# Two tiles of tokens at once in the second half of q and k and in the second mixer's q

## The chip, the cores and the metric

The kernel runs on one core of one Trainium2 chip. The metric is the device time of one execution in microseconds. The times of before are from three runs; a profile of one more execution gives the trace. Engines are called as in the profile: PE multiplies matrices, PEld is its weight load, DVE, ACT and POOL work on vectors, SP issues the DMAs.

## The reference

A decoder layer for 512 tokens of 1024 channels. One input projection of the normed input yields all parts; two attention mixers run on them; their outputs are gated, merged and projected. Cut to what matters here:

```python
h = rms_norm(x, norm_w)                       # (512, 1024)
proj = h @ w_in                               # all parts from one product
(q_a, k_a, v_a, z_a, q_b, kc, vc, ksl, vsl, kwn, vwn, gate_b, z_b, gate_m) = split(proj)
# first mixer: 8 heads of 64, causal softmax with a relative bias (512 tokens: every block is selected)
o_a = moba_mixer(rms_norm(heads(q_a), q_norm_a), rms_norm(heads(k_a), k_norm_a), heads(v_a), bias_a)
# compressed keys and values: windows of 32 tokens, a two-layer net
k_cmp = rms_norm(compress(heads(kc), ...), k_norm_cmp); v_cmp = compress(heads(vc), ...)
# second mixer: the same q against compressed, selected and window keys, three softmaxes, summed by gates
o_b = nsa_mixer(rms_norm(heads(q_b), q_norm_b), k_cmp, v_cmp, rms_norm(heads(ksl), ...), heads(vsl),
                rms_norm(heads(kwn), ...), heads(vwn), gate_b, bias_b)
y_a = o_a * silu(z_a);  y_b = o_b * silu(z_b);  g_m = sigmoid(gate_m)
merged = g_m[:, :1024] * (y_a @ w_branch_a) + g_m[:, 1024:] * (y_b @ w_branch_b)
x + merged @ w_out
```

## The kernel before

Products of the projections are made in three passes to keep float32's precision: each operand is split in a high part (rounded to the fast format, `hh` of the input, `wh` of a weight) and a low rest (`hl`, `wl`), and high x high, low x high and high x low are added up. ACT makes `wh` by a cast from the loaded weight `wr` (L402), DVE makes `wl` by a subtraction (L412). A "chunk" is 128 input channels by up to 512 columns; there are eight chunks (`KT`) to a group of columns.

There are four tiles of 128 tokens (`NT`). Two kinds of projection exist. A channel product (`gemm_chan`, for kc, vc, the z gates and the merge gates; accumulator `pgc`) holds weights still and streams all 512 tokens. A token product (`gemm_tok`; accumulator `pgt`) holds a tile of tokens still and streams 512 columns. The order of the projections is the list `qk0 v kc vc qk1 za0 kb za1 za2 qb za3 vb zb0 zb1 zb2 zb3`: qk1 is q and k of heads 4 to 7 of the first mixer, qb is the q of the second one. The first of the list, qk0, runs through `gemm_first`, with all four tiles at once in four accumulators (`pgf`). All others go tile by tile:

```python
def gemm_tok(name, emit, tags="gggg"):
    _, per, n = tlay[name]
    ws = W.take(KT // per, n)            # the split of all chunks is asked for here
    for t in range(NT):
        yield room(tags[t])              # an accumulator of this kind must be free
        ps = psum(tags[t], "pgt")
        ...                              # eight chunks x three products, each a step
                elif t == NT - 1:
                    W.split(W.i + i)     # in the last tile: ask for the next weights, a chunk a step
        with_rx(lambda t=t, ps=ps: emit(t, ps))
```

PSUM holds eight accumulators of one bank each: two of kind "g" (channel products, token products, branch products `pbr`), two "s" (scores `sps`), three "t" (small ones, and the compressor's hidden sum `hps`, which holds one for long) and one "o" (the attention outputs `O`).

When the four tiles of qk1 or qb end, `emit` starts a chain of steps for each: ACT evicts the accumulator to `nraw` with the token's scale (L772) and squares it (L774, one buffer `nxn` for all), DVE sums (L775), POOL takes the power -1/2 (L489), DVE multiplies by it and by the gains (L779, L786), ACT and DVE split the result into two half-precision parts (L795, L803, L796, L805, L1033), and after every second tile a DMA transposes it into `qkt` (L245).

Scores (L1094) are read from their bank by DVE (L1114), go through exponentials on ACT (L1125, L1132) and a rest on DVE (L1136), are transposed by DMA into `dst`, and are multiplied with v into `O` (L1168). In between, the compressor `compress_h` multiplies (L940, `hps`), copies its hidden sum to `hs` (L947 on ACT) and multiplies that (`pu`, L952).

All engines' instructions are put in order by a planner in the kernel itself, ahead of time: generators for scores, projections, compression, values and so on yield either a wait or the cost of what they issued, and the planner, with a clock of its own (`now`), takes at each step the one that may go on. An engine executes its queue in that order; semaphores make it wait where a result is missing.

Of the kernel before, what the change touches and what calls it, by code (L numbers as in the profile page):

```python
# [22 lines left out]
P = 128  # L23
NT = S // P
KT = D // P
# [33 lines left out]
SHARE_C = 100.0  # L59
LAG = 20000  # L60
MARGIN = 300
LATE_A = 1000
LATE_V = 2000
LATE_S = 1000
# [44 lines left out]
def hybrid_kernel(ctx: ExitStack, tc: tile.TileContext, x, x0, xT, wtok, wchan, gains, w1,  # L109
                  relone, wbr, wout, consts, out):  # L110
    nc = tc.nc
# [19 lines left out]
    now = [0.0]  # L131
# [26 lines left out]
    def cm(n):  # L158
        return 4.5 + 0.4427 * n
# [105 lines left out]
    def psum(tag, name, dt=F32):  # L265
        return alloc(tag, name, dt=dt)
# [9 lines left out]
    def room(*tags):  # L276

        def f():
            r = 0.0
            for tag in tags:  # L280
                if len(held[tag]) >= RES[tag][1]:
                    t = [z[0] for z in held[tag] if z[0] is not None]
                    if not t:
                        return None
                    r = max(r, min(t))
            return r
        return f
# [170 lines left out]
    first = alloc("dst", "x0", (P, NBLK * P // 2))  # L458
# [12 lines left out]
    hh = cp.tile([P, KT, S], F32R, name="hh")  # L471
    hl = cp.tile([P, KT, S], F32R, name="hl")
# [34 lines left out]
    for _ in range(NWARM):  # L507
        nc.tensor.matmul(pw[:, :P], warm[:, :1].to_broadcast([P, P]), warm[:, :1].to_broadcast([P, P]), start=True,
                         stop=True)
# [33 lines left out]
    def with_rx(fn):  # L543

        if "rx" in done:
            fn()
        else:
            rx_todo.append(fn)
# [45 lines left out]
    tlay, _ = tok_layout()  # L594
# [61 lines left out]
    for j in (5, 6, 2, 3, 4):  # L656
        tiles += right[j]
    W = Stream(tiles, NRAW - 2, lambda: wp.tile([P, WT], F32R, name=nm("wh"), tag="whi"),
               lambda: wp.tile([P, WT], F32R, name=nm("wl"), tag="wlo"))
# [10 lines left out]
    def gemm_tok(name, emit, tags="gggg"):  # L670
        _, per, n = tlay[name]
        ws = W.take(KT // per, n)
        for t in range(NT):
            yield room(tags[t])
            ps = psum(tags[t], "pgt")
            hs = [(hh[:, k, t * P:(t + 1) * P], hl[:, k, t * P:(t + 1) * P], None) for k in range(KT)]
            i = 0
            for c in mm3(ps[:, :n], hs, ws):
                yield c
                if not callable(c):  # L680
                    i += 1
                    if per == 2:
                        ahead((t + i / KT) / NT)
                    elif t == NT - 1:
                        W.split(W.i + i)
            with_rx(lambda t=t, ps=ps: emit(t, ps))

    def gemm_first(name, emit, tags="ggss"):

        _, per, n = tlay[name]  # L690
        ws = W.take(KT // per, n)
        ps = [psum(tag, "pgf") for tag in tags]
        for k in range(KT):
            for a, b in ((0, 0), (1, 0), (0, 1)):
                yield need(f"xl{k}" if a else f"xh{k}")
                if b or not a:
                    yield need((W, b, k // per))
                for t in range(NT):
                    nc.tensor.matmul(ps[t][:, :n], (hl if a else hh)[:, k, t * P:(t + 1) * P], ws[k][b],
                                     start=(k == a == b == 0), stop=(k == KT - 1 and b == 1))  # L700
                    if k == KT - 1 and b:
                        with_rx(lambda t=t: emit(t, ps[t]))
                yield cm(n) * NT
            W.split(W.i + k + 1)
# [112 lines left out]
    def proj_norm(name, first=False, tags="gggg"):  # L817
        two = []

        def emit(t, ps):  # L820
            if not t:
                qk_alloc(name)
            if t % 2 == 0:
                two[:] = [att(name, F32).bitcast(F16) for _ in range(2 + (name[:2] == "qk"))]
            n = 0 if name == "kb" else 2 if name == "qb" else 1
            q, k = two[:n], two[n:]
            ch = Chain(now[0] + 230)
            if name == "kb":
                e_ = sp.tile([P, 24], F32, name=nm("ge"), tag="ge", bufs=3)
                ch.do({"A": 164}, lambda e: e.activation(e_, ps[:, 256:280], AF.Exp, scale=nrx[:, t:t + 1]))  # L830
            norm(ch, ps, t, name, 4 if name == "kb" else 8, q, k)
            if name == "kb":
                def g1(e):
                    e.tensor_scalar(gate[:, 0, :, t], e_, 1.0, 1.0 / PS, op0=ALU.add, op1=ALU.mult)
                    e.reciprocal(gate[:, 1, :, t], gate[:, 0, :, t])
                ch.do({"D": 300}, g1)
            ch.mark(f"{name}.{t}")
        yield from (gemm_first(name, emit) if first else gemm_tok(name, emit, tags))

    def proj_v(name, tags="gggg"):  # L840
        toks[name], per, i = [None] * NT, 1 + (name == "vb"), int(name == "vb")
# [790 lines left out]
    class Run:  # L1632
        def __init__(r, gen, share, margin=MARGIN):
            r.gen, r.share, r.vt, r.wait, r.live, r.margin = gen, share, 0.0, lambda: 0.0, True, margin
# [10 lines left out]
    for k in range(KT):  # L1645
# [3 lines left out]
    now[0] = 3500.0  # L1649
    A, F, C, X, B, V = Run(scores(), SHARE_A, LATE_A), Run(gemms(), SHARE_F), Run(cmp(), SHARE_C, LATE_C), Run(x_rms(), 100.0), Run(prepare(), SHARE_B), Run(  # L1650
        values(), SHARE_V, LATE_V)
# [5 lines left out]
    while any(r.live for r in runs):  # L1657
        live = [r for r in runs if r.live]
        ws = [(r, r.wait()) for r in live]
# [88 lines left out]
```

## Time and profile before

| | |
|---|---|
| runs | 422.29 us median of 3 (421.83 to 422.44) |
| profiled execution | 422.54 us, of which the span in the trace is 420.5 us |
| PE, DVE, ACT, POOL busy | 411.8, 356.3, 297.9, 35.1 us |
| DMA queue of the kernel | 74.86 MB, 70.5% of the 16 engines' span |
| qk1's token products | from 64.57 us to 93.98 us |
| qb's token products | from 131.76 us, between other work |

A row of the timeline gives the start in microseconds, the duration, the engine, the line, the operation, output <- inputs, the shape and how many; in brackets the idle time of the engine before it and who ended it. Products are pipelined: the duration of one overlaps the next, so what a product costs is the distance from its start to the next one's. In the table of windows each engine has its busy time and instructions, and at the end of a row stand the granted clock of PE, the share of DMA and GB/s.

### The profile page before, as it was taken

How to read it: one execution, taken by the hardware profiler on the slowest of the kernel's cores; microseconds unless marked ns; L12 is line 12 of the kernel's file. 1: busy time of each engine (PE TensorE's matmuls, PEld its weight loads, DVE VectorE, ACT ScalarE, POOL GpSimd, SP SyncE). 2: the span in 40 equal slices, each digit the busy share in tenths (PEclk: the TensorE clock that was granted, in tenths of full speed). 3: DMA queues.
4: the chain of work that ended last, by engine and by line, in shares of the span. 5: the costliest groups of instructions: out<-in, count | busy, mean ns of one | idle time of the engine just before them, and what ended most of it. 6: DMA issues, size and time to landing. Idle time of an engine off the chain costs nothing.

```text
span 420.5 us, 7307 instructions
## 1 busy us (share of the span) xinstructions
PE 411.8 (98%) x2235; PEld 322.0 (77%) x2235; DVE 356.3 (85%) x933; ACT 297.9 (71%) x793; POOL 35.1 (8%) x37
## 2 busy tenths in 40 slices
PE   9999998999998999999999999999999999999996
PEld 7877875778976677897766777666777888888885
DVE  5967969999899987778999997899956967698993
ACT  7996748997797988727988897898943433445620
POOL 0015100123210033200000000000000000000000
PEclk9999999999999999999999999999999999999999
DMA  8951785688969988750878778889799597251232
GB/s 278 311 190 49 129 271 140 137 183 214 264 201 232 195 163 194 218 153 12 147 168 196 150 161 200 167 195 160 145 162 348 175 374 278 79 180 44 56 143 100
DMA packets 116693, 75.30 MB, mean 179 GB/s; under 512 B 89072, under 2 KB 92016, under 8 KB 116656
## 3 DMA queue, kind: packets, MB, share of 16 engines
q1 hardware_dynamic: 116656, 74.86, 70.5%
q8 instruction: 17, 0.28, 0.3%
q14 instruction: 20, 0.16, 0.1%
HBM read 51.11 MB, written 2.75 MB: 128 GB/s over the span
## 4 chain that ended last, share of the span: by engine, by line
PE 54%; DVE 23%; DMA 9%; ACT 5%; issue 5%; SPq 1%; POOL 1%; DVEq 0%; ACTq 0%; POOLq 0%
PE pgc L437 21%; PE pbr L437 9%; PE po L437 9%; PE pgt L437 8%; DMA wr<-in_wtok 5%; DVE sb L1114 4%; DVE wl L412 4%; DVE sb L1136 4%; DMA wr<-in_w 3%; PE O L1168 3%; PE sps L1094 3%; ACT wh L402 2%; DVE vl L412 1%; SPq L238 1%; DMA T<-rtab 1%
## 5 line engine op out<-in xcount | busy, mean ns | idle before, releaser
L437 PE MATMUL pgc<-hh,wh 128*128 128x512 f32 x208 | 87.1, 419 | 0.0
L412 DVE TENSOR_TENSOR wl<-wr,wh 128x512 fp32r<-128x512 f32 (+1 forms) x112 | 73.1, 669 | 11.8 <-ACT wh L402 11.6
L437 PE MATMUL pgc<-hh,wl 128*128 128x512 f32 x208 | 81.5, 392 | 0.0
L437 PE MATMUL pgc<-hl,wh 128*128 128x512 f32 x208 | 81.2, 390 | 0.0
L402 ACT CAST wh<-wr 128x512 fp32r<-128x512 f32 (+1 forms) x111 | 64.0, 599 | 11.2 <-DMA wr<-in_wtok 5.6
L1125 ACT ACTIVATE sb<-sb,sst 128x256 f32<-128x256 f32 (+3 forms) x96 | 53.2, 554 | 10.5 <-DVE sst L1114 10.2
L437 PE MATMUL pgt<-wh,hh 128*128 128x512 f32 (+2 forms) x160 | 58.3, 364 | 0.1
L437 PE MATMUL pgt<-wl,hh 128*128 128x512 f32 (+2 forms) x160 | 56.1, 351 | 0.5 <-DVE wl L412 0.4
L437 PE MATMUL pgt<-wh,hl 128*128 128x512 f32 (+2 forms) x160 | 55.8, 349 | 0.0
L1136 DVE SCALAR_TENSOR_TENSOR sb<-sb,sst 128x256 f16<-128x256 f32 (+3 forms) x96 | 51.1, 542 | 4.2 <-ACT sb L1132 3.9
L1114 DVE CUSTOM_DVE_ANT_0 sb<-sps,T,gst 128x512 f32<-128x512 f32 (+3 forms) x96 | 51.2, 541 | 3.5 <-PE sps L1094 1.6
L1132 ACT ACTIVATE sb<-sb,sst 128x256 f16<-128x256 f32 (+3 forms) x96 | 51.4, 552 | 4.0 <-DVE sst L1128 3.7
L437 PEld LDWEIGHTS pgc<-hh,wh 128*128 128x128 f32 x208 | 39.1, 188 | 8.6 <-issue 0.3
L437 PEld LDWEIGHTS pgc<-hh,wl 128*128 128x128 f32 x208 | 39.0, 188 | 8.6
L437 PEld LDWEIGHTS pgc<-hl,wh 128*128 128x128 f32 x208 | 39.2, 189 | 6.5
L1094 PE MATMUL sps<-qkt,qkt 128*128 128x512 f16 (+3 forms) x176 | 38.2, 310 | 1.6 <-DVE sst L1114 1.4
L489 POOL TENSOR_TENSOR nr<-nss,mhalf 128x8 f32<-128x8 f32 (+1 forms) x16 | 29.0, 1819 | 109.4 <-DVE nss L488 47.9
L437 PEld LDWEIGHTS pgt<-wl,hh 128*128 128x128 f32 x160 | 30.1, 188 | 5.5 <-DVE wl L412 1.6
L437 PEld LDWEIGHTS pgt<-wh,hh 128*128 128x128 f32 x160 | 30.2, 189 | 4.3 <-DVE X L912 0.4
L437 PEld LDWEIGHTS pgt<-wh,hl 128*128 128x128 f32 x160 | 30.2, 189 | 3.4
L1094 PEld LDWEIGHTS <-qkt 128*128 128x128 f16 x176 | 11.5, 98 | 21.4 <-issue 18.5
L437 PE MATMUL pbr<-yh,wh 128*128 128x512 f32 x64 | 26.4, 413 | 0.0
(229 smaller groups left out, 746.3 us busy)
## 6 DMA issues: line engine op xcount, KB each, us to landing
wr<-in_wchan SPq DMA_DIRECT2D x52, 256.0 KB, 3.8
wr<-in_wtok SPq DMA_DIRECT2D x36, 256.0 KB, 4.0
wq<-in_wout SPq DMA_DIRECT2D x36, 256.0 KB, 3.1
T<-rtab SPq DMA_DIRECT2D x16, 256.0 KB, 4.0
wr<-in_w SPq DMA_DIRECT2D x16, 256.0 KB, 3.7
wr<-in_wbr SPq DMA_DIRECT2D x16, 256.0 KB, 3.1
xr<-in_x SPq DMA_DIRECT2D x8, 256.0 KB, 5.3
x<-in_xT SPq DMA_DIRECT2D x7, 256.0 KB, 5.8
```

Source lines behind the costliest of these rows:

```text
L238: nc.sync.dma_start(out=dst, in_=src)
L402: e.copy(hi, raw)
L412: c.do(either(n), lambda e, hi=hi, lo=lo, raw=raw: e.tensor_sub(lo, raw, hi.bitcast(F32))).mark((w, 1, i))
L437: nc.tensor.matmul(dst, sts[i][a], mvs[i][b], start=(start and i == a == b == 0), stop=(stop and i == n - 1 and (a, b) == passes[-1]), ski ...
L489: c.do({"p": 700 + 150 * w}, lambda e: e.tensor_tensor(v(dst), v(ss), mhalf[:parts, :w], op=ALU.pow))
L1094: nc.tensor.matmul(sps[:, :n].rearrange("p (t n) -> p t n", n=P), qs, k4[:, x, j, :b + 1], start=not x, stop=bool(x))
L1114: e.tensor_tensor_reduce(z["sb"], sps[:, :L], T[:, S - L:], scale=nrunscale, scalar=3e38, op0=ALU.add, op1=ALU.min, accum_out=st[:, 0, b:b ...
L1125: c.do({"A": 279 + 0.834 * L}, lambda e: e.activation(z["sb"], z["sb"], AF.Exp, bias=st[:, 0, b:b + 1], scale=-1.0, accum_out=st[:, 1, b:b ...
L1132: e.activation(z["pp"][:, :L], z["sb"], AF.Copy, scale=s_)
L1136: c.do({"d": 59 + cd(L)}, lambda e: e.scalar_tensor_tensor(z["pp"][:, L:], z["sb"], s_, z["pp"][:, :L], op0=ALU.mult, op1=ALU.subtract))
L1168: nc.tensor.matmul(out, v[r][kb][:, vi * DH:(vi + 1) * DH], u.moving(kb, pi), start=p.first and kb == vi == pi == 0, stop=p.last and kb == ...
```

## The change

qk1 and qb go through a new function, `gemm_two`, which takes two tiles of tokens at once: for each chunk, the three passes are made for both tiles before the next chunk. The first two tiles take two accumulators of kind "t", the last two take both of kind "g". The next weights are asked for chunk by chunk over the whole second half. The chains of the two tiles of a half are put 1.5 us apart in the planner's time.

```diff
+STAG = 1500
+TWO = dict(qk1="ttgg", qb="ttgg")
...
+    def gemm_two(name, emit, tags):
+
+        _, per, n = tlay[name]
+        ws = W.take(KT, n)
+        for h in range(2):
+            ps = []
+            for tag in tags[2 * h:2 * h + 2]:
+                yield room(tag)
+                ps.append(psum(tag, "pgt"))
+            for k in range(KT):
+                yield ws[k][2].ready
+                for a, b in ((0, 0), (1, 0), (0, 1)):
+                    for i in range(2):
+                        t = 2 * h + i
+                        nc.tensor.matmul(ps[i][:, :n], (hl if a else hh)[:, k, t * P:(t + 1) * P], ws[k][b],
+                                         start=(k == a == b == 0), stop=(k == KT - 1 and b == 1))
+                yield cm(n) * 6
+                if h:
+                    W.split(W.i + k + 1)
+            for i in range(2):
+                Chain(now[0] + i * STAG).call(lambda t=2 * h + i, p=ps[i]: with_rx(lambda: emit(t, p)))
+
...
-        yield from (gemm_first(name, emit) if first else gemm_tok(name, emit, tags))
+        yield from (gemm_first(name, emit) if first else gemm_two(name, emit, TWO[name]) if name in TWO else gemm_tok(name, emit, tags))
```

Up to the first product of qk1 PE's order is unchanged, and behind the last attention output it is again the same; the other engines' orders part a little later and meet at about the same place. In between they are dealt anew. PE at the start of qk1, before (numbers are those of buffers):

```order
L437 MATMUL pgt182_865<-wh126_685,hh_108 128x512
L437 MATMUL pgt182_865<-wh126_685,hl_109 128x512
L437 MATMUL pgt182_865<-wl127_686,hh_108 128x512
L437 MATMUL pgt182_865<-wh129_693,hh_108 128x512
L437 MATMUL pgt182_865<-wh129_693,hl_109 128x512
L437 MATMUL pgt182_865<-wl130_694,hh_108 128x512
```

and PE at the same place after the change:

```order
L704 MATMUL pgt182_865<-wh126_685,hh_108 128x512
L704 MATMUL pgt183_866<-wh126_685,hh_108 128x512
L704 MATMUL pgt182_865<-wh126_685,hl_109 128x512
L704 MATMUL pgt183_866<-wh126_685,hl_109 128x512
L704 MATMUL pgt182_865<-wl127_686,hh_108 128x512
L704 MATMUL pgt183_866<-wl127_686,hh_108 128x512
L704 MATMUL pgt182_865<-wh129_693,hh_108 128x512
L704 MATMUL pgt183_866<-wh129_693,hh_108 128x512
```

A chunk of weights now serves six products in a row and two accumulators. Between these products stand scores: before, after 9, 12, 3, 9, 6, ... token products and mostly one pair at a time, now after 12, 18, 18, 12, 12, two pairs at a time.

PE at the end of qk1, where za0's channel product (`pgc`) begins, before (pgt239 is tile 3; tile 2 was pgt218, 24 products earlier):

```order
L437 MATMUL pgt239_1168<-wl179_862,hh_108 128x512
L437 MATMUL pgt239_1168<-wh180_863,hh_108 128x512
L437 MATMUL pgt239_1168<-wh180_863,hl_109 128x512
L437 MATMUL pgt239_1168<-wl181_864,hh_108 128x512
L437 MATMUL pgc265_1256<-hh_108,wh244_1183 128x512
```

and after the change (pgt201 is tile 2, pgt202 tile 3):

```order
L704 MATMUL pgt201_1011<-wh180_863,hl_109 128x512
L704 MATMUL pgt202_1012<-wh180_863,hl_109 128x512
L704 MATMUL pgt201_1011<-wl181_864,hh_108 128x512
L704 MATMUL pgt202_1012<-wl181_864,hh_108 128x512
L439 MATMUL pgc273_1270<-hh_108,wh215_1041 128x512
```

The two accumulators of kind "g" now both end here, and pgc273 takes over the one of pgt201. ACT's queue around the eviction that frees it, after the change (nraw217 and nraw224 are tiles 0 and 1 in their chains, xs the compressor's input, sb the scores):

```order
L404 CAST wh256_1216<-wr238_1141 128x280
L819 CAST qk1203_1019<-nraw217_1052 128x4x64
L404 CAST wh260_1234<-wr244_1170 128x280
L819 CAST qk1203_1019<-nraw224_1068 128x4x64
L796 ACTIVATE nraw268_1258<-pgt201_1011,rx_94 128x512
L1156 ACTIVATE sb245_1172<-sb245_1172,sst228_1074 128x256
```

and before, around the eviction of the last tile, which frees nothing that PE's next row needs:

```order
L803 CAST qk1200_958<-nraw204_962 128x2x64
L1033 CAST qk1200_958<-nraw204_962 128x2x64
L772 ACTIVATE nraw267_1263<-pgt239_1168,rx_94 128x512
L803 CAST qk1199_957<-nraw220_1054 128x2x64
L774 ACTIVATE nxn268_1264<-nraw267_1263 128x512
```

The eviction now stands behind the first splits of tiles 0 and 1, whose norms must be done. Where qb begins, PE's row `pu` (the compressor's next product, which waits for ACT's copy `hs`), before:

```order
L437 MATMUL pgc383_1776<-hl_109,wh339_1616 128x512
L437 MATMUL pgc383_1776<-hh_108,wl340_1617 128x512
L437 MATMUL pgt407_1878<-wh342_1625,hh_108 128x512
L437 MATMUL pgt407_1878<-wh342_1625,hl_109 128x512
L437 MATMUL pgt407_1878<-wl343_1626,hh_108 128x512
L952 MATMUL pu410_1893<-cst_89,hs395_1853 128x64 x2
```

and after the change:

```order
L439 MATMUL pgc387_1786<-hl_109,wh333_1592 128x512
L439 MATMUL pgc387_1786<-hh_108,wl334_1593 128x512
L439 MATMUL pgc387_1786<-hh_108,wh333_1592 128x512
L439 MATMUL pgc387_1786<-hl_109,wh333_1592 128x512
L439 MATMUL pgc387_1786<-hh_108,wl334_1593 128x512
L976 MATMUL pu390_1804<-cst_89,hs379_1750 128x64 x2
```

It moved ahead of qb's first product, and the last product of the hidden sum (`hps`), which stood six channel and token products and one pair of scores ahead of it, now stands fifteen channel products and two pairs ahead.

## The prediction

> **What bounds the kernel now.** I read the page first, then the table of windows, then the timeline of the TensorE row at the two places that the change touches. On the page, the busy shares, the slices and the chain of waits:
>
> ```profile
> PE 411.8 (98%) x2235; PEld 322.0 (77%) x2235; DVE 356.3 (85%) x933; ACT 297.9 (71%) x793; POOL 35.1 (8%) x37
> DVE  5967969999899987778999997899956967698993
> PEclk9999999999999999999999999999999999999999
> PE 54%; DVE 23%; DMA 9%; ACT 5%; issue 5%; SPq 1%; POOL 1%; DVEq 0%; ACTq 0%; POOLq 0%
> ```
>
> PE is busy 411.8 of 420.5 us at the full granted clock, so 8.7 us is idle; the rest can only shrink if products follow each other more closely. The table of windows (PE, PEld, DVE, ACT, POOL, then clock) says where the idle time is:
>
> ```profile
> 60.00:70.00 10.00, 9.59 (x46) 6.69 (x45) 9.80 (x31) 8.84 (x27) 0.00 (x0) 1.00 0.61 153
> 70.00:80.00 10.00, 8.69 (x39) 5.69 (x38) 9.81 (x32) 7.81 (x29) 0.00 (x0) 1.00 0.64 162
> 130.00:140.00 10.00, 8.53 (x43) 6.22 (x42) 9.63 (x28) 9.78 (x30) 1.01 (x1) 1.00 1.10 223
> 140.00:150.00 10.00, 9.21 (x62) 6.79 (x61) 9.24 (x35) 9.66 (x34) 0.76 (x1) 1.00 0.90 194
> 200.00:240.00 40.00, 39.94 (x242) 28.15 (x241) 39.73 (x124) 35.38 (x105) 0.00 (x0) 1.00 0.84 169
> ```
>
> 0.41 + 1.31 us stand where qk1 begins and 1.47 + 0.79 us where qb begins, each time with DVE above 92%: 4.0 us in exactly the stretches that the diff rewrites. Outside them PE hardly waits, even at 200 to 240 us where DVE has no idle time left. So the question is what these two stretches cost afterwards.
>
> **The change: products themselves, nothing.** 96 products of qk1 and 96 of qb remain, each with its own weight load, 128x512. What changes is that two accumulators alternate. The same alternation, over four, runs in gemm_first:
>
> ```profile
> 10.62 1.07 PE L699 MATMUL pgf<-wh,hh 128*128 128x512 f32 x4
> 11.53 1.07 PE L699 MATMUL pgf<-wh,hl 128*128 128x512 f32 x4
> 64.57 0.39 PE L437 MATMUL pgt<-wh,hh 128*128 128x512 f32 x1
> 64.80 0.39 PE L437 MATMUL pgt<-wh,hl 128*128 128x512 f32 x1
> ```
>
> Four in 0.91 us is 0.228 each; one tile at a time goes at 0.23. Term: 0.
>
> **Term 1, the weights of qk1's first tile.** Before, a chunk of weights is used up in three products (0.68 us), after in six (1.37 us). The first tile of qk1 in the timeline:
>
> ```profile
> 67.97 0.40 PE L437 MATMUL pgt<-wh,hl 128*128 128x512 f32 x1
> 68.75 0.50 PE L437 MATMUL pgt<-wl,hh 128*128 128x512 f32 x1 [0.39 <-DVE wl L412]
> 70.02 0.40 PE L437 MATMUL pgt<-wh,hl 128*128 128x512 f32 x1
> 70.53 0.49 PE L437 MATMUL pgt<-wl,hh 128*128 128x512 f32 x1
> 72.14 0.40 PE L437 MATMUL pgt<-wl,hh 128*128 128x512 f32 x1
> 73.65 0.38 PE L1094 MATMUL sps<-qkt,qkt 128*128 128x256 f16 x2 [1.12 <-DVE sst L1114]
> 74.11 0.50 PE L437 MATMUL pgt<-wh,hh 128*128 128x512 f32 x1
> 74.45 0.39 PE L437 MATMUL pgt<-wh,hl 128*128 128x512 f32 x1
> 68.02 1.28 DVE L412 TENSOR_TENSOR wl<-wr,wh 128x512 fp32r<-128x512 f32 x2
> 72.84 0.75 DVE L1114 CUSTOM_DVE_ANT_0 sb<-sps,T,gst 128x512 f32<-128x512 f32 x1
> ```
>
> From 67.97 to 68.75 is 0.78 instead of 0.23, from 70.02 to 70.53 0.51: 0.83 us lost to chunks 5 and 7, whose low halves DVE had just made. After, PE comes to chunk 5's low half at about 64.57 + 12 x 0.23 + 0.4 (a pair of scores) + 12 x 0.23 + 4 x 0.23 = 71.4; DVE has it at 68.7 (the first of the pair at 68.02). So both waits go: **-0.83**, between -0.83 and 0 (0 if DVE is 2.7 us later than before, which I see no reason for).
>
> **Term 2, the bank of the scores.** At 72.14 PE waits 1.51 - 0.23 = 1.28 us for a score bank, which DVE reads at 72.84 after four chunks of weights and two pairs of scores were asked of it within 8 us. After, two pairs of scores are issued in the same 8 us but with 30 token products between start and the second pair instead of 21, and the chunks stand ahead of the scores in DVE's queue. Walking DVE's queue with the durations above (0.6 a chunk, 0.4 to 0.7 a score), the third pair of scores finds its second bank some 0.4 us late. Term: **-0.9**, between -1.28 and +0.3 (three such waits of 0.4 us, less the 0.9 that I count).
>
> **Term 3, fewer returns from scores to tokens.** A token product that follows scores holds PE longer: 74.11 to 74.45 is 0.34, so 0.11 over the pitch. From the start of qk1 to the end of vb the order has 18 such returns, not 24, because scores now come in fours. Term: 6 x 0.11 = **-0.7**, between -0.7 and 0.
>
> **Term 4, a new wait: za0.** Both banks "g" now hold qk1's tiles 2 and 3, which end one product apart, and za0 needs one of them in the next row of PE. PE can't go on until ACT has evicted tile 2. How that is done now:
>
> ```profile
> 51.22 0.39 PE L437 MATMUL pgt<-wl,hh 128*128 128x512 f32 x1
> 51.65 0.69 ACT L855 ACTIVATE v<-pgt,rv 128x512 f16<-128x512 f32 x1 [1.12 <-PE pgt L437]
> 73.91 0.67 ACT L772 ACTIVATE nraw<-pgt,rx 128x512 f32<-128x512 f32 x1
> 87.48 0.40 ACT L795 CAST qk<-nraw 128x256 f16<-128x256 f32 x1
> 81.70 0.67 ACT L772 ACTIVATE nraw<-pgt,rx 128x512 f32<-128x512 f32 x1
> 91.94 0.39 ACT L795 CAST qk<-nraw 128x256 f16<-128x256 f32 x1
> ```
>
> Lower bound: a product's 0.39, 0.04 to ACT (51.61 to 51.65), 0.67 of eviction, some 0.06 back, less the two pitches in which PE goes on: 0.7 us. But in ACT's queue the eviction stands right behind the first cast of tile 1, which waits for that tile's norm on DVE and POOL. From eviction to that cast now takes 13.6 us (73.91 to 87.48) for tile 0 and 10.2 us (81.70 to 91.94) for tile 1. After, tiles 0 and 1 are evicted together at about 79 to 81, so tile 1's cast comes at 90 to 94.6, tile 2's eviction ends 1.1 us later, and PE is done with tile 3 at about 92.5: a wait of 0.7 to 3.2 us. What hid this before, the 5.4 us of the next tile, is gone. Term: **+1.4**, nearer to the lower end, since PE's own arrival has the same error as DVE's.
>
> **Term 5, heads 4 to 7.** Their first scores need the transposes of all of qk1:
>
> ```profile
> 88.99 0.67 ACT L772 ACTIVATE nraw<-pgt,rx 128x512 f32<-128x512 f32 x1
> 94.18 0.69 ACT L772 ACTIVATE nraw<-pgt,rx 128x512 f32<-128x512 f32 x1
> 108.51 2.91 SPq L245 DMA_TRANSPOSE qkt<-qk  x2
> qkt<-qk SPq DMA_TRANSPOSE x12, 3.3
> 112.96 0.60 PE L1094 MATMUL sps<-qkt,qkt 128*128 128x512 f16 x2
> ```
>
> Tiles 2 and 3 are evicted 5.2 us apart now, and the first of the two transposes issued from 108.51 lands some 3.3 us on, about a microsecond before the scores at 112.96. After, both tiles go through the single square buffer and DVE within about 1.5 us of each other, while PE has as many products left until those scores as before and four more. Term: **+0.6**, from 0 to 2.0 (a second norm's DVE rows behind the first).
>
> **Term 6, the start of qb.** Here PE waits for others:
>
> ```profile
> 130.49 0.40 PE L940 MATMUL hps<-vl,xs 128*128 128x256 f32 x2
> 132.22 0.40 PE L437 MATMUL pgt<-wl,hh 128*128 128x512 f32 x1
> 133.94 0.66 PE L952 MATMUL pu<-cst,hs 128*128 128x64 f32 x4 [1.32 <-ACT hs L947]
> 146.67 0.40 PE L1168 MATMUL O<-dst,v 128*64 128x512 f16 x1
> 147.86 1.66 PE L1168 MATMUL O<-dst,v 128*64 128x512 f16 x22 [0.79 <-DMA dst<-sb]
> ```
>
> 1.72 - 0.23 = 1.5 us for the copy of the compressor's hidden sum, and about 1.0 us (1.19 less a fifth) for a transpose of probabilities. In the new order 15 channel products and four of scores stand between the hidden sum and pu (about 4.0 us) instead of six and two (1.7 us), against 3.4 us that the copy takes from 130.49. And O stands 104 products behind the last score of its heads, not 91. If ACT and the transposes kept their lag, both waits would go: -2.5. But nothing fixes that lag: every queue is dealt anew there. I take 60%: **-1.6**, from -2.5 to +0.5 (the waits move and one returns).
>
> Sum: 0 - 0.83 - 0.9 - 0.7 + 1.4 + 0.6 - 1.6 = **-2.0 us**. What is gained stays gained: behind vb the two orders hold the same work to the end, and at 200 to 240 us DVE, though full, starts when PE's results come. The profiled execution took 422.5 us (420.5 and 2.0 around it), so 420.5; against the median of 422.3 it is **420.3 us**.
>
> A rule of the skill speaks against the change. The Trainium skill, "TensorE: Matmul & The Clock Gate", section "A second HAM failure mode: psum-queue depth-cycling", says that going round PSUM banks at every step can leave small idle gaps in which the clock gate drops to half. By it the sum would be far on the other side (rival D). The trace does not agree: pgf goes round four banks at 0.228 us, with PEclk at 9 tenths or more in every slice.
>
> **Rivals.** 0.2% (0.84 us) is about what a measurement of this kernel tells from no change.
> - A, all of terms 1, 2, 3 and 6 and only the least of 4: -0.83 - 1.28 - 0.7 - 2.5 + 0.7 = -4.6, **417.7 us**. For it: every wait named has a cause that the order takes away. Against: DVE stays full.
> - B, nothing: waits in a schedule dealt anew come back elsewhere. Terms 1 and 3 stay, 2 and 6 are zero, 4 and 5 as taken: +0.5, **422.8 us**, or about none.
> - C, slower: term 4 decides. If tile 1's norm takes as long behind tile 0's as tile 0's does today plus POOL and DVE again, some 17 us, the eviction ends at 98 and PE stands 5.5 us. With the other terms as taken that is +2.1, **424.4 us**. It turns the sign from a wait of 3.4 us on, and is measurably slower from 4.3 us.
> - D, the clock falls to half over the 192 products: 192 x 0.228 = +44 us, **466 us**. Against it stands every pgf row.
>
> **Chances.** The forecast, from 418.5 to 421.4: 0.45. A: 0.15. B: 0.22. C: 0.17. D: 0.01. So faster 0.60, same 0.22, slower 0.18. Range: from A's better end, 417.4, to midway into C, 423.6; the forecast's own is 418.5 to 421.4.
>
> **What would show it.** Right: no PE wait on wl in qk1's first half, no wait for sst near 72; a new wait in front of za0's first pgc, released by ACT nraw, of 0.7 to 3 us; PE busy above 9.5 of 10 at 130 to 150. Wrong: that wait over 4 us, or new waits for scores or hps near 110 to 150 that add up to what is saved.

## The result, and the profile after

| | before | after |
|---|---|---|
| median of four runs beside each other | 422.06 us (420.48 to 422.44) | 427.89 us (425.90 to 429.21) |
| profiled execution, its span | 422.54, 420.5 us | 427.74, 425.6 us |

The ratio is 1.0142 (95% interval 1.0118 to 1.0166): the change makes the kernel 6 us slower, where 2 us less were forecast. One execution of e7, below, was granted 0.56 of the clock and took 681 us; it is left out of that run's time and ratio. The page of after, in the parts that were shown of before:

```profile
PE 414.1 (97%) x2235; PEld 324.3 (76%) x2235; DVE 355.7 (84%) x931; ACT 298.2 (70%) x795; POOL 32.0 (8%) x37
DVE  4977969999799977768999989988965877698993
PEclk9999999999999998999999999999999999999999
PE 51%; DVE 22%; ACT 13%; DMA 7%; issue 6%; SPq 0%; DVEq 0%; ACTq 0%; POOL 0%; POOLq 0%
```

The work is the same, and still PE is busy 2.3 us longer and idle 2.8 us longer. The 8 in PEclk, in the slice from 159.6 to 170.2 us, is new, and in the chain ACT has 13% instead of 5%. The table of windows, after:

```profile
60.00:70.00 10.00, 9.93 (x49) 7.24 (x48) 9.83 (x30) 8.51 (x26) 0.00 (x0) 1.00 0.64 160
70.00:80.00 10.00, 9.43 (x45) 7.13 (x44) 9.83 (x31) 6.89 (x24) 0.00 (x0) 1.00 0.66 163
130.00:140.00 10.00, 10.00 (x48) 7.45 (x47) 9.97 (x31) 10.00 (x35) 0.00 (x0) 1.00 0.96 209
140.00:150.00 10.00, 10.00 (x50) 7.43 (x50) 8.29 (x33) 9.20 (x31) 0.55 (x1) 1.00 1.11 199
150.00:160.00 10.00, 9.33 (x63) 7.20 (x62) 8.81 (x25) 7.65 (x22) 3.25 (x2) 1.00 0.82 157
160.00:170.00 10.00, 7.62 (x43) 5.14 (x42) 7.66 (x15) 9.77 (x27) 0.00 (x0) 0.85 1.06 227
```

and two rows of before that the prediction had no use for:

```profile
150.00:160.00 10.00, 10.00 (x48) 8.13 (x47) 9.19 (x29) 8.58 (x23) 3.68 (x4) 1.00 0.83 148
160.00:170.00 10.00, 10.00 (x68) 7.90 (x68) 6.91 (x13) 8.83 (x24) 3.65 (x1) 1.00 0.95 230
```

The four rows in which before was idle have nearly filled up: 0.64 us idle instead of 1.72 at 60 to 80, none instead of 2.26 at 130 to 150. The loss lies right behind them, at 150 to 170, where before had no idle time: 3.05 us idle, and a stretch at half the clock. Two rows of the timeline of after bound the stretches, vb's last token product and the first output product; in before they stood at 186.49 and 351.65 us:

```profile
190.15 0.28 PE L439 MATMUL pgt<-wl,hh 128*128 128x256 f32 x1
356.74 0.62 PE L439 MATMUL po<-wh,mh 128*128 128x512 f32 x2
```

So PE reaches the end of vb 3.66 us later, and needs 166.59 instead of 165.16 us from there, 1.43 us more, for the second mixer's heads. From the first output product both take 65.3 us to PE's last product.

PE at the end of qb (timeline of after):

```profile
162.07 0.61 PE L704 MATMUL pgt<-wl,hh 128*128 128x512 f32 x2
163.92 0.50 PE L964 MATMUL hps<-vh,xs 128*128 128x256 f32 x2 [1.23 <-ACT vh L404]
164.65 0.51 PE L964 MATMUL hps<-vl,xs 128*128 128x256 f32 x2 [0.23 <-DVE vl L414]
165.08 0.40 PE L1192 MATMUL O<-dst,v 128*64 128x512 f16 x1
166.41 2.94 PE L1192 MATMUL O<-dst,v 128*64 128x512 f16 x23 [0.92 <-DMA dst<-sb]
170.30 0.42 PE L439 MATMUL pgc<-hh,wh 128*128 128x512 f32 x1
```

with ACT's cast `vh` and its evictions of qb's last two tiles, and the last transpose that O needs on SP's queue:

```profile
163.25 0.61 ACT L404 CAST vh<-wr 128x512 fp32r<-128x512 f32 x1
165.58 0.68 ACT L796 ACTIVATE nraw<-pgt,rx 128x512 f32<-128x512 f32 x1
167.47 0.68 ACT L796 ACTIVATE nraw<-pgt,rx 128x512 f32<-128x512 f32 x1
163.31 1.17 SPq L247 DMA_TRANSPOSE dst<-sb  x1
```

PE has qb's last product under way at 162.30, but tiles 2 and 3 hold both banks of kind g until ACT evicts the first at 165.58 to 166.26. So za3, for which nothing else is missing, can't be given to PE, and the order puts the hidden sum and the attention output ahead of it. PE stands in front of each in turn. Before, qb's tiles ended one after another, 24 token products apart, so a bank came free while PE still had the next tile's products.

A second thing differs there. The same place in before (PE, the four transposes that the same O needs, and the last part of the probabilities on DVE), and that part after the change:

```profile
162.86 0.40 PE L437 MATMUL pgt<-wl,hh 128*128 128x512 f32 x1
163.19 1.82 PE L1168 MATMUL O<-dst,v 128*64 128x512 f16 x24
164.94 0.50 PE L437 MATMUL pgc<-hh,wh 128*128 128x512 f32 x1
155.06 5.25 SPq L245 DMA_TRANSPOSE dst<-sb  x4
154.97 0.35 DVE L1136 SCALAR_TENSOR_TENSOR sb<-sb,sst 128x128 f16<-128x128 f32 x1
161.67 0.34 DVE L1160 SCALAR_TENSOR_TENSOR sb<-sb,sst 128x128 f16<-128x128 f32 x1
```

In before the four transposes were issued by 160.31 and O began without a wait; in after the last one is issued at 163.31, and DVE ends the last part of the probabilities at 162.01 instead of 155.32. So PE has less to fill the time with, and what it waits for also comes later.

### The profile page after: what moved, and what is told of

The parts are those of the page before. It is cut to its first block, busy times and chain, and to the rows that moved or that the text cites. A ratio compares the mean times of both kernels' runs of the same rounds, so it can differ in the third digit from the quotient of the medians.

```text
span 425.6 us, 7312 instructions
## 1 busy us (share of the span) xinstructions
PE 414.1 (97%) x2235; PEld 324.3 (76%) x2235; DVE 355.7 (84%) x931; ACT 298.2 (70%) x795; POOL 32.0 (8%) x37
## 4 chain that ended last, share of the span: by engine, by line
PE 51%; DVE 22%; ACT 13%; DMA 7%; issue 6%; SPq 0%; DVEq 0%; ACTq 0%; POOL 0%; POOLq 0%
PE pgc L439 15%; PE po L439 9%; PE pgt L439 8%; PE pbr L439 7%; PE pgf L723 5%; DMA dst<-sb 4%; DVE sb L1138 4%; ACT sb L1149 4%; DVE sb L1160 4%; DVE wl L414 3%; ACT sb L1156 3%; PE O L1192 2%; ACT wh L404 2%; DMA wr<-in_w 2%; DMA T<-rtab 1%
## 5 line engine op out<-in xcount | busy, mean ns | idle before, releaser
L1149 ACT ACTIVATE sb<-sb,sst 128x512 f32<-128x512 f32 (+3 forms) x96 | 53.3, 556 | 10.8 <-DVE sst L1138 10.3
L1156 ACT ACTIVATE sb<-sb,sst 128x512 f16<-128x512 f32 (+3 forms) x96 | 50.9, 553 | 5.2 <-DVE sst L1152 4.7
L1160 DVE SCALAR_TENSOR_TENSOR sb<-sb,sst 128x512 f16<-128x512 f32 (+3 forms) x96 | 50.9, 544 | 4.2 <-ACT sb L1156 3.9
L491 POOL TENSOR_TENSOR nr<-nss,mhalf 128x8 f32<-128x8 f32 (+1 forms) x16 | 25.6, 1608 | 83.2 <-DVE nss L490 82.9
L439 PE MATMUL pgt<-wh,hh 128*128 128x512 f32 (+2 forms) x96 | 31.2, 325 | 0.0
L439 PE MATMUL pgt<-wh,hl 128*128 128x512 f32 (+2 forms) x96 | 30.8, 321 | 0.0
L439 PE MATMUL pgt<-wl,hh 128*128 128x512 f32 (+2 forms) x96 | 30.8, 321 | 0.0
L439 PE MATMUL pbr<-yh,wl 128*128 128x512 f32 x64 | 25.1, 392 | 0.0
L439 PE MATMUL pbr<-yl,wh 128*128 128x512 f32 x64 | 24.9, 390 | 0.0
L704 PE MATMUL pgt<-wh,hh 128*128 128x512 f32 x64 | 20.9, 408 | 0.0
```

Source lines behind the costliest of these rows:

```text
L439: nc.tensor.matmul(dst, sts[i][a], mvs[i][b], start=(start and i == a == b == 0), stop=(stop and i == n - 1 and (a, b) == passes[-1]), ski ...
L491: c.do({"p": 700 + 150 * w}, lambda e: e.tensor_tensor(v(dst), v(ss), mhalf[:parts, :w], op=ALU.pow))
L704: nc.tensor.matmul(ps[i][:, :n], (hl if a else hh)[:, k, t * P:(t + 1) * P], ws[k][b], start=(k == a == b == 0), stop=(k == KT - 1 and b = ...
L1149: c.do({"A": 279 + 0.834 * L}, lambda e: e.activation(z["sb"], z["sb"], AF.Exp, bias=st[:, 0, b:b + 1], scale=-1.0, accum_out=st[:, 1, b:b ...
L1156: e.activation(z["pp"][:, :L], z["sb"], AF.Copy, scale=s_)
L1160: c.do({"d": 59 + cd(L)}, lambda e: e.scalar_tensor_tensor(z["pp"][:, L:], z["sb"], s_, z["pp"][:, :L], op0=ALU.mult, op1=ALU.subtract))
```

## The experiments

Tags name the kinds of bank that a group's four tiles take: "ttgg" is the change's. Beside medians, the table behind them has PE's lost time: for each of PE's products the distance from its start to the next one's, less the pitch of its shape (0.227 us for 512 columns of float32), summed, as a difference to before, over three stretches: the first 10 us, which no kernel here changes, from there to vb's last token product, and the rest.

**e1 to e4: which half, and which banks.**

```diff
-TWO = dict(qk1="ttgg", qb="ttgg")
+TWO = dict(qk1="ttgg")                # e1
+TWO = dict(qb="ttgg")                 # e2
+TWO = dict(qk1="ttgg", qb="tggt")     # e3
+TWO = dict(qk1="ttgg", qb="ggtt")     # e4
```

> Only qk1 runs two tiles at once; qb goes tile by tile as before. Theory (the end of qb): what was lost lies between 152 and 171 us of the span, where after the change both banks of kind g hold qb's last two tiles, so that PE cannot take za3 and stands in front of the hidden sum and the attention outputs with nothing to fill the wait, and the clock then drops. With qb tile by tile that end comes apart again: about 5.3 us less there, some of it given back because the new waits at qk1's end (1.7 us at za0) and the later order (some 2 us between 254 and 280 us) stay: 423 to 425 us, no half clock near 165 us. Rival (any new dealing of this stretch costs some microseconds, since the vector engines have no slack in it): 426 to 428 us, with waits of PE in other places.

Measured: 426.64 us, ratio 1.0107 (1.0075 to 1.0139). The rival's range. With qb tile by tile PE doesn't stand at its end, but the wait at za0 is there, and at 138.92 PE waits 1.91 us for a weight's low half in qb:

```profile
138.92 0.50 PE L439 MATMUL pgt<-wl,hh 128*128 128x512 f32 x1 [1.91 <-DVE wl L414]
```

> Only qb runs two tiles at once; qk1 goes tile by tile as before. Theory (the end of qb): the start is that of before to 130 us, the two waits at qb's start go (1.5 to 2 us gained), and the end of qb brings the loss, 3 to 5 us between 152 and 171 us: 423.5 to 426 us. Rival (any new dealing costs): 426 to 428 us. Second rival (the loss came down from qk1's new waits, 1.7 us at za0 and a later start of heads 4 to 7): about 420.5 us, faster than before.

Measured: 429.17 us, 1.0163 (1.0135 to 1.0190), worse than any of the three expected. Here the order has za3 right behind qb, and PE waits 3.1 us for its bank (PE's row, then ACT's eviction, which stands behind casts and squares of weights; PE's last product had begun some 0.2 us after 158.43):

```profile
162.18 0.50 PE L439 MATMUL pgc<-hh,wh 128*128 128x512 f32 x1 [3.13 <-ACT nraw L796]
161.44 0.68 ACT L796 ACTIVATE nraw<-pgt,rx 128x512 f32<-128x512 f32 x1
```

Twice in this kernel the clock goes to half, behind this wait and behind one of 2.37 us at 265 to 268 us.

> As after the change, but qb's four tiles take banks t, g, g, t: one bank of kind g is free when qb ends. PE's order is that of after to the end of qb; there 6 + 6 products of za3 now stand ahead of the hidden sum's second pair and of the attention output. Theory (the end of qb): the waits at 162 to 166 us (1.4, 0.4 and 1.1 us) shrink to under 0.5 us together, the clock stays at 1.00, and the order of the second mixer's heads is again that of before, so the 2 us at 254 to 280 us go too: 420.5 to 422.5 us. Rival (the vector engines are late there by themselves, because PE has outrun them by 1.5 to 2 us, and it waits for them a little further on): the 3 us of waits reappear between 165 and 180 us, 425 to 427 us.

Measured: 423.31 us, 1.0039 (1.0017 to 1.0060). That is between the two ranges, 0.8 us above the theory's. Still this is the cleanest pair: PE's order is that of after up to the end of qb. PE and the last transpose there:

```profile
163.55 0.39 PE L439 MATMUL pgc<-hh,wh 128*128 128x512 f32 x1
164.91 0.51 PE L964 MATMUL hps<-vh,xs 128*128 128x256 f32 x2
165.64 0.50 PE L964 MATMUL hps<-vl,xs 128*128 128x256 f32 x2 [0.22 <-DVE vl L414]
167.93 1.82 PE L1192 MATMUL O<-dst,v 128*64 128x512 f16 x24
163.89 1.17 SPq L247 DMA_TRANSPOSE dst<-sb  x1
```

The transpose is issued as late as in after (163.31), so ACT, DVE and SP are no faster. PE has twelve products of za3 to fill the time, and O begins without a wait. From vb's end on, PE's, DVE's, ACT's and SP's orders are those of before (PE's last 1300 products, from 176.6 us of before on), and so is the time: 187.95 to 353.08 us, 165.13 us.

```profile
187.95 0.28 PE L439 MATMUL pgt<-wl,hh 128*128 128x256 f32 x1
353.08 0.39 PE L439 MATMUL po<-wh,mh 128*128 128x512 f32 x1
```

> As after the change, but qb's first two tiles take both banks g and its last two both banks t. Theory (the end of qb): za3 has its bank, yet the order now puts twelve products of the hidden sum in a row and the attention output ahead of the last 24 products of qb, so part of the wait may stay in the middle of qb: 421.5 to 425 us, the clock at 1.00 if no gap over about 1 us follows another. Rival (the vector engines are late by themselves): 425 to 428 us.

Measured: 428.97 us, 1.0165 (1.0136 to 1.0193), above the expected range. qb's start now needs both banks of kind g, which za2's products hold, so the order puts four pairs of scores nearly in a row ahead of it, and PE waits for score banks, first in the row below and then 0.68 us more; in qb's first products it waits 0.56 us until DVE has emptied za2's accumulator (`zs`), the second bank of kind g:

```profile
135.05 0.38 PE L1118 MATMUL sps<-qkt,qkt 128*128 128x256 f16 x2 [1.44 <-DVE sst L1138]
```

Half the clock follows, from 136 to 143 us. The place of the wait moved from qb's end to its start. That both banks are needed at one moment costs at either.

**e5: both groups with a bank left.**

```diff
+TWO = dict(qk1="ttgt", qb="tggt")
```

> Both groups with one bank of kind g free when they end: qk1 takes t, t, g, t, and qb takes t, g, g, t. Theory (a bank held at the end is what costs): against qb's t, g, g, t alone (423.3 us) the 1.7 us wait in front of za0 goes too, because za0 has the bank that vc left: 421 to 422 us, no clock drop, if the new order brings no gap of its own. Rival (what PE saves at za0 it waits for at the first scores of heads 4 to 7 or at qb's start, since the vector engines set the pace there): 423 to 425 us, with a new gap of 1 to 2 us between 110 and 150 us.

Measured: 422.27 us, 1.0012 (0.9991 to 1.0034): no difference to before, and between the two ranges. za0's first product follows qk1's last at the pitch, 0.45 us after the row of two:

```profile
92.35 0.62 PE L704 MATMUL pgt<-wl,hh 128*128 128x512 f32 x2
92.80 0.39 PE L439 MATMUL pgc<-hh,wh 128*128 128x512 f32 x1
```

But a wait of 1.01 us for `vl` follows at 95.57 and one of 1.46 us for the compressor's `gt` at 149.63, which the rival had foreseen.

**e6: is it the clock?** Six more products, by zeros, where PE waits for `vh`:

```diff
+if name == "qb" and h and k == KT - 1 and b:
+    for _ in range(6):
+        nc.tensor.matmul(ps[0][:, :n], warm[:, :1].to_broadcast([P, P]),
+                         warm[:, :1].to_broadcast([P, n]), start=False, stop=False)
```

> As after the change, with six extra products by zeros in qb's last accumulator just ahead of its last two products: the result does not change, and PE is busy for about 1.3 us of the 1.4 us that it waited for ACT's vh at 162.3 us. All other queues are as after the change. Theory (the gaps take the clock down, and the half clock costs 1.7 us on top of them): no idle time of 2 us or more within 4 us is left, the clock stays at 1.00, 425.9 to 426.5 us. Rival (the half clock has another cause, or costs nothing because PE would wait for others anyway): 427.5 to 428.5 us, and the half clock is there again.

Measured: 427.74 us, 1.0134 (1.0098 to 1.0169). The half clock is gone in the profiled execution (of the other five, one has a mean clock of 0.996, which such a stretch would give), the time stays. O's first product follows its transpose later (167.24 us, after 1.26 us of waiting), and the burst that took from 166.41 to 169.28 us in after then takes from 167.24 to 168.98. One row of after and one of e6 (windows):

```profile
168.00:169.00 1.00, 1.00 (x8) 0.54 (x4) 0.60 (x2) 1.00 (x3) 0.00 (x0) 0.50 2.34 103
168.00:169.00 1.00, 1.00 (x18) 0.64 (x14) 0.69 (x1) 1.00 (x3) 0.00 (x0) 1.00 2.29 176
```

So the half clock costs about 1.1 us over O alone, where it falls; but it is not what makes the change slow. Why e6 gained nothing was not settled: ACT, DVE and PE had been about 0.35 us later than in after since 151 to 155 us, ahead of the added products, by which the profiled executions of one order can differ.

**e9, e10: is it ACT's queue?** The eight squares of vb's weights, which stand ahead of `vh` and of the evictions:

```diff
-  e.activation(y, z.bitcast(F32), AF.Square, scale=g, accum_out=acc)
+  ... if m > 256 else e.activation(acc, z[:, :1].bitcast(F32), AF.Square, scale=g)
```

> As after the change, but the eight squares that ACT makes of vb's weights between 158 and 167 us (0.51 us and 0.19 us for the sum, each) are taken of one column only (some 0.1 us each), so vb's scale is not computed; the order of all queues is the same. Theory (PE stands there because ACT's queue, with vh and the evictions behind the squares, is late): vh comes 2 to 3 us earlier, so the 1.4 and 0.4 us in front of the hidden sum go, the bank for za3 comes some 4 us earlier, and the clock stays at 1.00: 424 to 426 us. Rival (the transposes on SP's queue, not ACT, end last there: PE waits for the attention output all the same): 427 to 428.5 us, with over 2 us of wait at O.

Measured: 427.52 us, 1.0152 (1.0131 to 1.0172). The theory falls; the rival's time and place hold, though its wait at O is 1.69 us and not over 2:

```profile
162.22 0.50 PE L965 MATMUL hps<-vh,xs 128*128 128x256 f32 x2 [0.40 <-ACT vh L404]
163.65 0.50 PE L965 MATMUL hps<-vl,xs 128*128 128x256 f32 x2 [0.93 <-DVE vl L415]
166.17 2.88 PE L1193 MATMUL O<-dst,v 128*64 128x512 f16 x23 [1.69 <-DMA dst<-sb]
```

The wait for ACT went from 1.23 to 0.40 us, those for DVE and the transpose from 0.23 and 0.92 to 0.93 and 1.69: 3.02 us in all instead of 2.38. That ACT was relieved is plain: `vh` came 1.7 us earlier, the first eviction 2.3 us. ACT, DVE and the transposes are late together, and relieving one shows the next.

> The counterpart: the kernel before with the same eight squares of one column only (vb's scale is not computed), the order of all queues the same. Theory: before, PE has za3 and token products ahead of whatever waits for ACT there, so 4 us less on ACT bring nothing: 421 to 422.5 us, as before. Rival (ACT bounds this stretch with or without the change): 418 to 420 us.

Measured: 421.48 us, 1.0002 (0.9984 to 1.0020), as the theory had it.

**e7 and e11: qb alone, with a bank left** (`TWO = dict(qb="tggt")`, twice).

> Only qb runs two tiles at once, and takes t, g, g, t. Against qb alone with t, t, g, g (429.2 us), theory (a bank held at the end): the 3.1 us gap at 159 to 162 us, where za3 has no bank, goes, and with it the half clock behind it (1.7 us): 424.4 us at most; if the 2.3 us gap and the half clock at 265 to 271 us, which the later order brings, go too, about 420.5 us. Rival (the vector engines set the time at the end of qb, a bank or none): 427 to 429 us, with the gap a little further on.

> The kernel with qb alone two tiles at once, in t, g, g, t, once more for its profile. It took 427 us where the theory of the bank gave 424.4 at most. If the bank is not what costs, a gap of 2 us or more stands again between 150 and 175 us; if the bank was free in time and the loss is the later order's, the gaps stand behind 250 us, 3 to 5 us of them, with a half clock.

Measured: 426.86 us (median of five), 1.0113 (1.0078 to 1.0147), and in e11, from two executions, 425.04 us, 1.0084 (1.0055 to 1.0112); both lie between e7's two ranges. By e11's trace PE has lost 1.1 us less than before up to vb's end, with one wait of 1.60 us ahead of 163.12, for the compressor's `kr`, and no half clock; 3.4 us are lost behind it, in waits of 0.3 to 1 us for scores and outputs between 229 and 315 us. So the bank was free in time, and the later order takes the gain and more.

**e8, e12, e19: new orders without the change.** Numbers of the planner, in the kernel before: MARGIN 500 (e8), LATE_V 2300 (e12), LATE_A 900 (e19). Each says how many ns a result must have been ready, by the planner's clock, before the step that needs it gets a turn ahead of others: LATE_A for scores, LATE_V for values, MARGIN for projections and whatever has no number of its own.

> A control without the change: the kernel before with one number of its planner altered (MARGIN 500 instead of 300), which deals PE's order anew from the end of qk1 on and keeps all projections tile by tile. Theory (the banks): no accumulators are held at an end, so nothing like the loss: 420.5 to 423 us, gaps under 2 us, the clock at 1.00. Rival (the order of before is a lucky one, and any other costs some microseconds): 424 to 428 us.

> A second control without the change: the kernel before with LATE_V 2300 instead of 2000, which deals the order anew already in qk1. The first control cost 3 us (425.0 us), with 0.5 to 1.3 us of waits in new places. If the order of before is a lucky one, this one lies at 423 to 427 us too; if the first control was an accident, at 420.5 to 422.5 us.

> A third control without the change: the kernel before with LATE_A 900 instead of 1000. If a new order as such costs (the order of before is a favourable one): 423.5 to 427 us, with new waits of 1 us or more at the start of qb or behind 250 us. If the first two controls were accidents: 420.5 to 422.5 us.

Measured: 424.96 us, 1.0073 (1.0044 to 1.0101); 426.21 us, 1.0106 (1.0081 to 1.0130); 422.78 us, 1.0029 (1.0002 to 1.0055). The first two lie where a lucky order puts them, e19 between its two ranges. In these three, a new order costs 1 to 5 us with no change in the work. e12's worst row is a score bank at qb's start, with half the clock behind it:

```profile
138.78 0.60 PE L1094 MATMUL sps<-qkt,qkt 128*128 128x512 f16 x2 [2.41 <-DVE sst L1114]
```

**e13 to e16: banks against order.** The change's banks with MARGIN 500 (e13) and with LATE_A 1200 (e14), e5's banks with LATE_A 1200 (e15) and with MARGIN 500 (e16).

> The change with MARGIN 500: PE's order is that of the change up to the end of qb, with the same banks, and another one behind it. Theory (banks): the loss between 152 and 171 us stays: 426 to 429 us. Rival (the later order makes a good part of the loss): 423.5 to 425.5 us, with less than 0.5 us of waits where 2 us stood between 254 and 280 us.

> The change with LATE_A 1200 instead of 1000: another order from qk1 on, the same banks (t, t, g, g); at the end of qb again the hidden sum and the attention output stand ahead of za3. Theory (banks): 425 to 429 us, with a wait in front of za0 and 2 us or more of waits at the end of qb. Rival (the order alone decides): anything from 421 to 429 us, without a pattern.

> Banks held apart (qk1 t, t, g, t and qb t, g, g, t) with LATE_A 1200. Theory (banks): 421 to 424 us, 3 us or more below the run with t, t, g, g under the same planner. Rival (the order alone decides): within 1.5 us of that run, or above it.

> Banks held apart with MARGIN 500; the order up to qb's end is that of the run with banks apart (422.3 us), behind it PE's rows are dealt anew in part. Theory (banks): 421 to 424 us, 3 us or more below the change with MARGIN 500. Rival (the later order decides): over 424 us.

Measured: 430.86 us, 1.0241 (1.0215 to 1.0267); 426.71, 1.0153 (1.0117 to 1.0190); 425.40, 1.0114 (1.0089 to 1.0140); 422.47, 1.0031 (1.0010 to 1.0053). Ratios to before, by setting:

| | as given | MARGIN 500 | LATE_A 1200 |
|---|---|---|---|
| without the change | 1 | 1.0073 | none (e17) |
| both g's held (ttgg, ttgg) | 1.0142 | 1.0241 | 1.0153 |
| a bank left (ttgt, tggt) | 1.0012 | 1.0031 | 1.0114 |

The kernel before with LATE_A 1200 (e17), which was to be the control of the last column, can't be built: in its order the engines wait for each other without end. e16 came out as its theory had it; e13 is worse than either of its ranges; e14 lies in its theory's range, but its waits at qb's end are 1.53 us and not 2. Held banks cost 1.3%, 2.1% and 0.4% against a bank left: the first two clear of noise, but under LATE_A 1200 the difference is 1.3 us instead of the 3 us that the theory asked for, which is the rival's range. The kernels of a pair differ in their later order too, which in the controls above cost 0.3% to 1.1%, so these ratios alone don't part the two causes; the last table of this section does so in part. Under MARGIN 500 two tiles at once with a bank left came out ahead of tile by tile (1.0031 against 1.0073), but the intervals overlap, as those under LATE_A 1200 do. The largest single wait but one (e2's) is that for the bank in front of za0 in e14:

```profile
96.64 0.50 PE L439 MATMUL pgc<-hh,wh 128*128 128x512 f32 x1 [3.08 <-ACT nraw L796]
```

**e18: a version that might beat both** (`TWO = dict(qk1="ttgt")`).

> Only qk1 two tiles at once, in t, t, g, t; qb tile by tile. Theory (banks): no wait in front of za0, none of the both-g kind at the end of qb; the two waits at qk1's start go (some 2 us), one of 1.2 us at the hidden sum near 94 us comes: 420.5 to 422.5 us. Rival (any new order costs, as the controls did): 424 to 427 us.

Measured: 425.86 us, 1.0110 (1.0072 to 1.0147). The theory falls again behind vb: up to there it has lost 0.6 us less than before, then it loses 4.1 us more, of which one row has two and a half clock follows:

```profile
264.38 1.93 PE L1192 MATMUL O<-dst,vb 128*64 128x512 f16 x15 [1.99 <-DMA dst<-sb]
```

No version run here beats before; the best, e5, is level with it. The lost time of the profiled executions, in us against before (the sum is the difference of the spans):

| kernel | first 10 us | to vb's end | behind it |
|---|---|---|---|
| after | +0.6 | +3.1 | +1.4 |
| e13, after with MARGIN 500 | +0.3 | +3.2 | +3.6 |
| e14, after with LATE_A 1200 | +0.5 | +1.2 | +1.5 |
| e1, qk1 ttgg | +0.6 | +2.5 | +2.5 |
| e2, qb ttgg | +0.1 | +2.1 | +4.4 |
| e4, qk1 ttgg, qb ggtt | +0.4 | +4.7 | +1.4 |
| e3, qk1 ttgg, qb tggt | +0.9 | +0.5 | 0.0 |
| e5, qk1 ttgt, qb tggt | +0.3 | -1.0 | +1.4 |
| e16, e5 with MARGIN 500 | 0.0 | -2.5 | +0.9 |
| e15, e5 with LATE_A 1200 | +0.6 | +1.2 | +1.0 |
| e11, qb tggt | +0.5 | -1.1 | +3.4 |
| e18, qk1 ttgt | 0.0 | -0.6 | +4.1 |
| e8, e12, e19, no change | +0.2, +0.6, +0.6 | -0.2, +0.9, -0.9 | +2.6, +1.8, +1.3 |

Two things stand in it. To vb's end, the first six, which hold both g's at the end or the start of qb, or of qk1 alone, lose 2.1 to 4.7 us, e14 1.2; with a bank left in every group (e5, e16, e15, e11, e18) it is -2.5 to +1.2, as without the change (-0.9 to +0.9), and e3, which keeps the wait at za0, lies between. The pair under LATE_A 1200 is the exception: e14, with the banks held, and e15, with a bank left, both lose 1.2 us. Behind vb, the order of before is the best of the table: every other one loses 0.9 to 4.4 us, with the change and without it, and only e3, which has that order, loses nothing. These are single executions: e1 has the order of after behind vb, and lost 2.5 us there where after lost 1.4.

## Why the prediction was wrong, point by point

- **Products themselves, 0.** Right. At the end of qk1 in after, pairs start 0.46 us apart, 0.23 us each, and the clock is 1.00 there:

```profile
92.68 0.62 PE L704 MATMUL pgt<-wh,hl 128*128 128x512 f32 x2
93.14 0.61 PE L704 MATMUL pgt<-wl,hh 128*128 128x512 f32 x2
95.30 0.50 PE L439 MATMUL pgc<-hh,wh 128*128 128x512 f32 x1 [1.54 <-ACT nraw L796]
```

  So rival D, and what it takes from the Trainium skill ("TensorE: Matmul & The Clock Gate", section "A second HAM failure mode: psum-queue depth-cycling"), is not borne out by these products.
- **Terms 1 and 2, -1.73.** Counted as the prediction does, from start to start less the pitch, 2.13 us became 0.73: -1.40. The mechanism was right. The waits for wl are gone; of the wait for the score bank 0.57 us of idle time stay, at 78.03. A wait that no term had, of 0.62 us at 90.49 for a low half `vl` of the compressor's weights, takes part of it back.
- **Term 3, -0.7.** Right: PE's first product behind each of the 24 returns from scores took 2.93 us over its pitch in sum, behind the 18 of after 2.09, so -0.84.
- **Term 4, +1.4.** Right: from 93.14 to 95.30 is 2.16, less two pitches 1.70 us, released by ACT's eviction. e5 takes it away.
- **Term 5, +0.6.** Too high: the first scores of heads 4 to 7 begin at 115.68, 0.30 us after a token product of 0.13 us pitch at 115.38, so they cost 0.17 us.
- **Term 6, -1.6.** Too small, even: 2.26 us of idle time at 130 to 150 us are gone. (60% of 2.5 is 1.5; the sum has 1.6.)
- **The step that failed** is the one behind the sum: "What is gained stays gained: behind vb the two orders hold the same work to the end". Every sign of being right that the prediction names is there, and none of its signs of being wrong; the loss lies behind the last place that they name. At qb's last product after had lost 1.1 us less than before, counting from 10 us on; from there to vb's end it lost 4.2 us more, and 1.4 us more behind vb. So the step failed in two places. First, the walk stopped at qb's start. Term 4 had named the mechanism, both banks of kind g ending together with ACT's eviction late in its queue, and priced it at za0; qb ends in the same two banks, in front of za3, and that end was not walked. There it cost 3.05 us of idle time at 150 to 170 us and 3.4 us at half the clock. e3, in which only qb's banks differ, brings the time down by 1.0% of the kernel, to 423.3 us; in the profiled executions 2.6 us of that come up to vb's end and 1.4 behind it. The traces do not settle why the last probabilities of that O came 6.7 us later than in before; in e3 they come later still, and PE has za3 to fill the time. Second, the same work behind vb does not mean the same time: it is dealt in another order, and that alone cost 1.4 us here (2.5 us in e1, which has the same order there) and up to 4.4 us elsewhere. The sentence on DVE at 200 to 240 us did not show that the order is without price; there was no row on it, and it needed a range of its own.
- **Rival B** said that waits in a schedule dealt anew come back elsewhere, which is what e8, e12 and e19 do without the change, and with it e5. It was priced as if they could only take back what was gained. Rival C had the right side and the right mechanism at the wrong group: its wait at za0 stayed at 1.70 us.

Of the 5.1 us between the profiled executions, 0.6 lie in the first 10 us, which the change doesn't touch, 3.1 up to vb's end and 1.4 behind it. How much of the 3.1 us the half clock makes is not settled: O's burst shows 1.1 us of it, e18's executions with and without it differ by 2.2 us (below), while e6 without it was no faster.

## What to carry to other kernels

Two accumulators that fill together also end together. Before giving them the last banks of a kind, ask which row of the matmul engine comes next, whether it needs a bank of that kind, and how late the evicting engine's queue is there; and ask it at every place where the change is made. Where the order is dealt by a planner, measure first what a neutral new deal costs (1 to 5 us in the three controls here): a forecast narrower than that has no ground, and a gain smaller than that can't be credited to the edit.

## What the runs showed of the hardware that was not expected

PE's clock falls to half behind quite short gaps, in the middle of a busy kernel, for about 3.4 us each time (twice that in e4). After, by the windows:

```profile
166.00:167.00 1.00, 0.59 (x7) 0.39 (x9) 0.81 (x2) 1.00 (x5) 0.00 (x0) 0.97 0.78 207
167.00:168.00 1.00, 1.00 (x16) 0.91 (x12) 0.57 (x3) 1.00 (x3) 0.00 (x0) 0.50 0.93 306
169.00:170.00 1.00, 1.00 (x5) 0.72 (x4) 0.39 (x1) 0.81 (x2) 0.00 (x0) 0.50 0.20 18
170.00:171.00 1.00, 1.00 (x6) 0.89 (x5) 0.00 (x0) 0.07 (x1) 0.00 (x0) 0.83 1.10 294
```

By their clocks, (1 - 0.97) + 3 x 0.5 + (1 - 0.83) is 1.70 us lost, 3.4 us at half. What went before it was 2.38 us of idle time in three pieces within 4 us, none over 1.23 us. In e1 a single gap of 1.91 us was enough, in e18 one of 1.99 us; the 3.08 us in e14, the longest but one, brought no half clock in the profiled execution, nor did the 1.54 us at za0 in after. The same order comes with the half clock and without it: 3.4 us at half in 424 us make a mean clock of 0.996, and three of e18's six executions have 0.995 or 0.996 and took 427.2 us on average, the other three, at 1.000, 425.0 us; in e1 one of six has it, in e14 the three that were not profiled have 0.992 to 0.996. The Trainium skill, "TensorE: Matmul & The Clock Gate", section "Part 1: The HAM clock gate (the "warmup" mystery)", has a free-running window of 3413 ns, which agrees with the length and would explain why a longer gap can go without. Its advice to keep gaps under about 3 us, in the section "Why this matters for your kernels", differs from these rows, and the rows decide here: the half clock came behind less than 2 us.
